# Output projection of a hybrid encoder block: the first product is copied into the residual stream, and its residual is added by the first of three adding DMAs

## The chip, the cores and the metric

The kernel runs on one core of a Trainium2 chip. The metric is the device time of one execution in microseconds (us); lower is better. The engines of the core are named as the profile names them: PE (matrix products), DVE (VectorE), ACT (ScalarE), POOL (GpSimd) and SP (a queue that only issues DMAs).

## What is computed

One layer of an encoder block on 512 tokens with 1024 features, all in float32:

```python
h = rms_norm(x, mix_norm_g)
proj = h @ w_in            # feeds three mixers and their merge gates
merged = g_ml * (y_ml @ w_br_ml) + g_na * (y_na @ w_br_na) + g_xa * (y_xa @ w_br_xa)
x = x + merged @ w_out                                           # the output projection
x = x + conv_glu_ffn(rms_norm(x, ffn_norm_g), w_ffn_up, ...)     # the feed-forward part
return rms_norm(x, final_norm_g)
```

The change lies in the line `x = x + merged @ w_out`: a product of 512x1024 by 1024x1024, the sum with the old `x` (the residual), and the start of the RMS norm that comes next.

## The kernel before, in words

Every float32 product is made of three matmuls (`mm3`, lines 223 to 226): both operands are split into a high and a low part, and high by high, high by low and low by high are summed in PSUM. ACT makes the high part by a copy, DVE the low part by a subtraction. For weights of the other stages these are the pairs at lines 184 and 185; in the output projection they are lines 1238 and 1239 for `w_out` and its sums, and lines 1132 and 1134/1136 for the blocks of `merged`.

The output projection uses seven products instead of eight (Strassen's scheme in Winograd's form). `merged` and `w_out` are cut into two by two blocks; each of the products p1, p5, p2, p6, p3, p7, p4 (`ORDER_O`, in this order) multiplies a sum of blocks of `merged` (256 tokens by 512 features) by a block, or a sum of blocks, of `w_out` (512 by 512). The sums on the weight side were made earlier by DMAs and lie in the tensor `tout`. The sums on the side of `merged` are made in place by DVE (lines 1119, 1121, 1129, 1130). One product is 24 matmuls: four steps `k`, two token tiles `t`, three matmuls each (lines 1438 to 1461).

A product's result is a PSUM tile of 128x1024 (two banks of 512), from a pool of two such tiles (`w2p`, names `at`). The products alternate between the two, so a product may begin only when the result of the product two places ahead of it has been read: p3 begins when p2's result has been read, p4 when p3's has.

The new residual stream lies in two tiles, one for each half of the tokens: `xtu[0]` (named `u_5188` in the rows below) and `xtu[1]` (`u_5189`). `cells((r, c))` is a quarter: token half `r`, feature half `c`, as 128x2x512. The function `wide_adder` builds the quarters. A running sum `Q` starts with p1 and takes p6 and p7. `residual(c)` issues on POOL a DMA that adds a quarter of the old `x` (`xtok` in HBM) to what stands in `cells(c)`. Before the change this goes as follows:

- p1: ACT copies p1 to `Q` (line 1180).
- p5: ACT copies p5 into both quarters of the right half, and POOL issues the adding DMA of each (lines 1186, 1187, 1171).
- p2: DVE writes p2 + `Q` into quarter (0, 0) (line 1182), and POOL then issues that quarter's adding DMA (lines 1183, 1171).
- p6, p3, p7 and p4 follow with sums by DVE (lines 1189, 1191, 1193, 1175, 1163). Quarter (1, 0) takes its `x` by a plain load (line 1422).

Once a token tile is done, ACT forms the sums of its squares in two halves (`squares`, line 1203), DVE adds them (line 1213), POOL takes the power -0.5 (line 1208), ACT scales the tile (`normed`, line 1399, tiles `z`), and PE transposes it for the feed-forward part (`turn`, line 1414). The table `todo` (lines 1428 to 1436) says at which step each of these functions is called: `add("p1")` at step 1 of p5, `add("p2")` at step 1 of p6, `turn(0)` for the first 256 tokens at step 2 of p4. A scheduler then orders the instructions of each engine from its own estimates, so that neighbours on an engine need not stand in the order of the code. Each engine works its list off in order: an instruction that waits holds up all behind it.

Meanwhile SP loads what comes next: the sums in `tout` for p7 and p4 (line 1230), and the first weights of the feed-forward part (`wr<-wflat`, line 160) through a ring of three buffers that it shares with some blocks of `w_out`. ACT splits those weights at line 184.

Of the kernel before, what the change touches and what calls it, by code (L numbers as in the profile page):

```python
# [13 lines left out]
AF = mybir.ActivationFunctionType  # L14
ALU = mybir.AluOpType
# [87 lines left out]
def hybrid_block(ctx, tc, xg, xT, xtok, memT, wflat, wout, wdn, vecs, gbias, nabias, out):  # L103
    nc = tc.nc
    V, A, G, PE, SY = nc.vector, nc.scalar, nc.gpsimd, nc.tensor, nc.sync
# [13 lines left out]
    def nm(s):  # L119
        uid[0] += 1  # L120
        return f"{s}_{uid[0]}"

    def unit(dt=F32):
        return up.tile([P, UNIT], dt, tag="unit", name=nm("u"))
# [7 lines left out]
    def mmps():  # L132
        return mmp.tile([P, 512], F32, tag="mm", name=nm("mm"))
# [271 lines left out]
    def proj(key, XHs, XLs, n=S, at={}, ps=None):  # L405

        ws = weights(key)
        k0 = 0 if ps is None else 1
        if ps is None:
            ps = mmps()  # L410
        for k in range(k0, KT):
            mm3(ps[:, :n], ws[k][0], ws[k][1], XHs[k], XLs[k], k == 0, k == KT - 1)
            if k in (1, 3, 5):
                flush()
            if k in at:
                at[k]()
        return ps
# [63 lines left out]
    for f in range(4):  # L481
        ps = ps_k[f] if f < 2 else proj(("mlk", f), XH, XL)
# [27 lines left out]
    for c in range(3):  # L510
        n, nk = TMC[c], TMK[c]
        pss = [(mmps if c % 2 else atps)() for _ in range(NT)]
        for h in range(KT // nk):
            ws = weights(("tm", c, h))
            for t in range(NT):
                tsl = slice(t * P, (t + 1) * P)
                for k in range(nk):
                    kk = nk * h + k
                    ps = pss[t][:, :n]
                    mm3(ps, XH[kk][:, tsl], XL[kk][:, tsl], ws[k][0], ws[k][1], kk == 0, kk == KT - 1)  # L520
        for t in range(NT):
            ps = pss[t]
# [619 lines left out]
    def cells(c):  # L1142
        return xtu[c[0]][:, :2 * D].rearrange("p (t n) -> p t n", t=2)[:, :, c[1] * S:(c[1] + 1) * S]
# [23 lines left out]
    def wide_adder(banks, Q):  # L1167

        def residual(c):
            r0, c0 = c[0] * 2 * P, c[1] * S  # L1170
            G.dma_start(cells(c), xtok[r0:r0 + 2 * P, c0:c0 + S].rearrange("(t p) n -> p t n", p=P), accum_op=ALU.add)

        def add(name, c=None):
            if c is not None:
                V.tensor_tensor(cells(c), cells(c), Q[0], op=ALU.subtract if c[1] else ALU.add)
                return
            ps = banks[name].rearrange("p (t n) -> p t n", t=2)
            if name == "p1":
                Q.append(unit()[:, :2 * S].rearrange("p (t n) -> p t n", t=2))
                A.activation(Q[0], ps, AF.Copy)  # L1180
            if name == "p2":
                V.tensor_tensor(cells((0, 0)), ps, Q[0], op=ALU.add)
                residual((0, 0))
            if name == "p5":
                for r in range(2):
                    A.activation(cells((r, 1)), ps, AF.Copy)
                    residual((r, 1))
            if name == "p6":
                V.tensor_tensor(Q[0], ps, Q[0], op=ALU.add)
            if name == "p3":  # L1190
                V.tensor_tensor(cells((0, 1)), ps, cells((0, 1)), op=ALU.add)
            if name == "p7":
                V.tensor_tensor(Q[0], Q[0], ps, op=ALU.subtract)

        return add
# [52 lines left out]
    def step(n=1):  # L1248
        quota[0] += n
        while quota[0] >= 1 and gens:  # L1250
            try:
                next(gens[0])
                quota[0] -= 1
            except StopIteration:
                gens.pop(0)
        if not gens:
            quota[0] = 0.0
# [5 lines left out]
    def paced(key, rate=RB):  # L1263
        return proj(key, XH, XL, at={k: lambda: step(rate / 4) for k in (1, 3, 5)})

    xq = unit()
    for f in range(4):
        ps = proj(("xaq", f), XH, XL)
# [3 lines left out]
    for f in range(4):  # L1272
        ps = paced(("o", f), RN if f else RB)
# [15 lines left out]
    for f in range(4):  # L1289
        ps = proj(("memk", f), MH, ML, M, at={3: lambda: step(RM / 2)})  # L1290
# [15 lines left out]
    for f in range(4):  # L1306
        ps = paced(("naq", f), RN)
        V.tensor_tensor(nq[:, f * S:(f + 1) * S].rearrange("p (b r c) -> p b r c", r=ROWS, b=4), rv(ps), rv(rb),
                        op=ALU.mult)
        step(RN / 4)  # L1310
    for f in range(4):
        ps = paced(("nak", f), RN)
# [12 lines left out]
    for br in range(3):  # L1325
# [19 lines left out]
        for fp in range(4):  # L1345
# [16 lines left out]
            for i in range(2):  # L1362
                f = 2 * fp + i
                ps = mmps()
# [236 lines left out]
    banks, Q = {}, []  # L1601
# [196 lines left out]
```

## Time and profile before

| what | value |
|---|---|
| median of 3 runs | 858.2 us (857.5, 858.2, 859.56) |
| the profiled execution's own time | 858.97 us |
| its span in the profile | 857.2 us |
| PE, share of the span busy | 848.3 us, 99% |
| DVE | 622.6 us, 73% |
| ACT | 480.2 us, 56% |
| POOL | 133.0 us, 16% |

The span runs from the first to the last instruction of the program; the profiled execution took 1.8 us more than that. Times in rows of the profile count from the start of the span. A row of the timeline gives start, duration, engine, line, operation, `out<-in`, how many instructions were merged into the row, and in square brackets the idle time of the engine ahead of it with what ended it. The output projection takes from about 460 to 502 us.

### The profile page before, as it was taken

Reading aid. Unit: us, or ns where it says so; the run is one execution under the profiler, and the core shown is the slowest. Engines: PE = TensorE matmul, PEld = TensorE weight load, DVE = VectorE, ACT = ScalarE, POOL = GpSimd, SP = SyncE. Lnnn points to the kernel's source line nnn. Section 1 sums busy time; section 2 is a strip of 40 time slices with the busy share of each in tenths; the row PEclk is TensorE's granted clock in tenths of the full one; section 3 lists DMA queues with packets and bytes.
Section 4 is the critical chain, followed back from the end, with each engine's and each line's share of the span. In section 5 each row is a group of like instructions: output and inputs, shape, how many; then the busy total and the mean of one; then the engine's idle time right before and its main releaser. Section 6 shows DMA issues by size and latency. Waiting matters only on the chain.

```text
span 857.2 us, 12114 instructions
## 1 busy us (share of the span) xinstructions
PE 848.3 (99%) x4175; PEld 716.8 (84%) x4175; DVE 622.6 (73%) x1277; ACT 480.2 (56%) x988; POOL 133.0 (16%) x245
## 2 busy tenths in 40 slices
PE   9999999999999999999999999999999999999996
PEld 7898889988888888888888888888888888888885
DVE  7774698987567758898769967475758666694784
ACT  7663467675446658888735674343434444463463
POOL 0101100010127561600000111030213110001101
PEclk9999999999999999999999999999999999999999
DMA  8233642595664444544442844487869672477942
GB/s 280 81 108 123 185 154 84 158 290 154 179 196 127 114 125 131 157 142 132 146 178 98 221 147 145 152 286 277 262 217 352 203 243 99 135 251 257 381 166 99
DMA packets 53982, 155.00 MB, mean 181 GB/s; under 512 B 6872, under 2 KB 11992, under 8 KB 53344
## 3 DMA queue, kind: packets, MB, share of 16 engines
q1 hardware_dynamic: 30912, 101.37, 34.8%
q0 software_dynamic: 22576, 52.46, 20.8%
q8 instruction: 33, 0.54, 0.3%
q10 hardware_dynamic: 432, 0.39, 0.1%
q14 instruction: 29, 0.24, 0.1%
HBM read 132.68 MB, written 29.90 MB: 190 GB/s over the span
## 4 chain that ended last, share of the span: by engine, by line
PE 94%; DVE 2%; DMA 2%; ACT 1%; issue 1%; POOL 0%; SPq 0%; POOLq 0%
PE mm L224 25%; PE mm L225 25%; PE mm L226 25%; PE at L225 4%; PE at L226 4%; PE at L224 4%; DMA u<-xtok 1%; PE at L990 1%; PE at L971 1%; DVE u L1239 1%; DMA wr<-wflat 0%; PE at L952 0%; PE at L953 0%; PE at L773 0%; PE at L821 0%
## 5 line engine op out<-in xcount | busy, mean ns | idle before, releaser
L224 PE MATMUL mm<-u,wh 128*128 128x512 f32 (+1 forms) x859 | 330.1, 385 | 0.4 <-ACT wh L184 0.3
L225 PE MATMUL mm<-u,wh 128*128 128x512 f32 (+1 forms) x859 | 327.7, 382 | 0.0
L226 PE MATMUL mm<-u,wl 128*128 128x512 f32 (+1 forms) x859 | 327.7, 382 | 0.0
L184 ACT ACTIVATE wh<-wr 128x512 fp32r<-128x512 f32 (+2 forms) x240 | 149.8, 628 | 236.6 <-PE mm L225 198.8
L185 DVE TENSOR_TENSOR wl<-wr,wh 128x512 fp32r<-128x512 f32 (+2 forms) x242 | 164.2, 683 | 84.2 <-ACT wh L184 83.5
L226 PEld LDWEIGHTS mm<-u,wl 128*128 128x128 f32 x859 | 161.4, 188 | 31.4 <-DVE wl L185 0.2
L224 PEld LDWEIGHTS mm<-u,wh 128*128 128x128 f32 x859 | 161.3, 188 | 30.9 <-ACT wh L184 0.7
L225 PEld LDWEIGHTS mm<-u,wh 128*128 128x128 f32 x859 | 161.6, 188 | 30.4 <-DVE u L231 0.4
L548 POOL DMA_DIRECT2D u<-nav_d x128 | 62.7, 531 | 55.6 <-PE at L990 23.0
L1132 ACT ACTIVATE u<-u 128x1024 fp32r<-128x1024 f32 (+1 forms) x28 | 27.5, 998 | 32.0 <-PE mm L226 9.0
L225 PE MATMUL at<-wl,u 128*128 128x512 f32 (+2 forms) x130 | 44.0, 338 | 0.0
L226 PE MATMUL at<-wh,u 128*128 128x512 f32 (+2 forms) x130 | 43.8, 337 | 0.0
L224 PE MATMUL at<-wh,u 128*128 128x512 f32 (+2 forms) x130 | 43.7, 337 | 0.0
L1134 DVE TENSOR_TENSOR u<-u,u 128x1024 fp32r<-128x1024 f32 (+1 forms) x21 | 23.7, 1134 | 13.6 <-ACT u L1132 13.5
L1580 DVE TENSOR_TENSOR u<-mm,s 128x512 f32<-128x512 f32 x22 | 15.2, 689 | 25.1 <-PE mm L226 23.6
L225 PE MATMUL mm<-wl,u 128*128 128x512 f32 x80 | 31.3, 391 | 0.0
L224 PE MATMUL at<-u,u 128*128 128x512 f32 x80 | 31.2, 390 | 0.0
L226 PE MATMUL mm<-wh,u 128*128 128x512 f32 x80 | 31.2, 390 | 0.0
L226 PE MATMUL at<-u,u 128*128 128x512 f32 x80 | 31.1, 389 | 0.0
L225 PE MATMUL at<-u,u 128*128 128x512 f32 x80 | 31.1, 389 | 0.0
L224 PE MATMUL mm<-wh,u 128*128 128x512 f32 x80 | 31.0, 390 | 0.0
L1488 POOL DMA_DIRECT2D tsp<-u x22 | 15.6, 709 | 96.5 <-ACT u L1483 89.1
(365 smaller groups left out, 1333.4 us busy)
## 6 DMA issues: line engine op xcount, KB each, us to landing
wr<-wflat SPq DMA_DIRECT2D x117, 512.0 KB, 3.8
u<-wdn POOLq DMA_DIRECT2D x11, 1024.0 KB, 9.4
tsp<-u POOLq DMA_DIRECT2D x22, 512.0 KB, 6.9
u<-tsp POOLq DMA_DIRECT2D x10, 1024.0 KB, 6.0
tdn<-u POOLq DMA_DIRECT2D x11, 512.0 KB, 6.3
tout<-wout POOLq DMA_DIRECT2D x4, 1024.0 KB, 9.7
nab<-nabias SPq DMA_DIRECT2D x16, 256.0 KB, 2.8
u<-nav_d POOLq DMA_DIRECT2D x128, 32.0 KB, 2.8
```

The source lines that it names most:

```text
L184: A.activation(h[:, u:v], src, AF.Copy)
L185: V.tensor_tensor(l[:, u:v], src, h[:, u:v].bitcast(F32), op=ALU.subtract)
L224: PE.matmul(ps, lh, rh, start=start, stop=False)
L225: PE.matmul(ps, lh, rl, start=False, stop=False)
L226: st["mm"] = PE.matmul(ps, ll, rh, start=False, stop=stop).ins
L548: G.dma_start(vw[r * 32:(r + 1) * 32, i * 256:(i + 1) * 256], nav_v[hf, r, CW[b]:CW[b] + 32, hp * 256:(hp + 1) * 256])
L971: PE.transpose(pt[:, j * P:(j + 1) * P], sm[:, j * P:(j + 1) * P], ident)
L990: PE.matmul(py[:, bl * 256:(bl + 1) * 256], vw[:, c:c + P], pp[bl][:, hf * 256:(hf + 1) * 256], start=hf == 0, stop=hf == 1)
L1132: st["oh"] = A.activation(r3(h), src, AF.Copy, scale=scale).ins
L1134: V.tensor_tensor(r3(l), src, r3(h).bitcast(F32), op=ALU.subtract)
L1488: G.dma_start(tsp[:, x, :, ks].rearrange("q p n -> p q n"), hl[0][:, x])
L1580: V.tensor_tensor(ur, pu, c, op=ALU.mult)
```

## The change

ACT now copies p1 twice: first into quarter (0, 0) of the residual stream, then to `Q` as before. Right behind the first copy that quarter's adding DMA is issued, ahead of the two of the right half. When p2 is done, DVE adds p2 to what stands in the quarter, in place, and no DMA follows.

```diff
             if name == "p1":
                 Q.append(unit()[:, :2 * S].rearrange("p (t n) -> p t n", t=2))
+                A.activation(cells((0, 0)), ps, AF.Copy)
+                residual((0, 0))
                 A.activation(Q[0], ps, AF.Copy)
             if name == "p2":
-                V.tensor_tensor(cells((0, 0)), ps, Q[0], op=ALU.add)
-                residual((0, 0))
+                V.tensor_tensor(cells((0, 0)), ps, cells((0, 0)), op=ALU.add)
```

In the changed kernel the lines behind this place move down by one: the copy to `Q` is line 1182, the sum with p2 line 1184, the copies of p5 line 1187, the splits of `w_out` lines 1239 and 1240, the squares line 1204.

On POOL the adding DMA of quarter (0, 0) now stands ahead of the other two. On SP the two loads of `tout` for p4 now stand ahead of the first load of feed-forward weights, not behind it. PE's list is the same. ACT and DVE are ordered anew in two places. The names in the rows: `u_2700` and `u_2701` are the blocks of `merged`; `u_5312` or `u_5314` and the like are the split parts of `w_out`; `wr_5362` and `wr_5364` before, `wr_5363` and `wr_5365` after, are the first two weight blocks of the feed-forward part in the ring.

ACT before, from the split of p7's first half of weights to the first two sums of squares:

```order
L1238 ACTIVATE u_5312<-wr_5251 128x1024
L184 ACTIVATE wh_5442<-wr_5362 128x512
L184 ACTIVATE wh_5446<-wr_5362 128x512
L1132 ACTIVATE u_5321<-u_2700 128x1024
L1238 ACTIVATE u_5334<-wr_5269 128x1024
L1238 ACTIVATE u_5350<-u_5293 128x1024
L1132 ACTIVATE u_5359<-u_2700 128x1024
L184 ACTIVATE wh_5465<-wr_5364 128x512
L1238 ACTIVATE u_5375<-u_5293 128x1024
L1132 ACTIVATE u_5378<-u_2701 128x1024
L1203 ACTIVATE s_5389,y_5388<-u_5188 128x512
L1203 ACTIVATE s_5392,y_5391<-u_5188 128x512
```

The same stretch of ACT after the change:

```order
L1239 ACTIVATE u_5314<-wr_5253 128x1024
L1132 ACTIVATE u_5323<-u_2700 128x1024
L1239 ACTIVATE u_5335<-wr_5271 128x1024
L1239 ACTIVATE u_5351<-u_5295 128x1024
L1132 ACTIVATE u_5360<-u_2700 128x1024
L184 ACTIVATE wh_5443<-wr_5363 128x512
L184 ACTIVATE wh_5447<-wr_5363 128x512
L184 ACTIVATE wh_5466<-wr_5365 128x512
L184 ACTIVATE wh_5470<-wr_5365 128x512
L1239 ACTIVATE u_5376<-u_5295 128x1024
L1132 ACTIVATE u_5379<-u_2701 128x1024
L1204 ACTIVATE s_5390,y_5389<-u_5188 128x512
```

The four splits of feed-forward weights (line 184) now stand together, ahead of the last two copies for p4 (`u_5376`, `u_5379`). Before, two stood further ahead, one directly ahead of these copies, and the fourth behind the first two sums of squares.

DVE before, from a low part for p6 to the sum with p2 and two more low parts:

```order
L1239 TENSOR_TENSOR u_5234<-wr_5147,u_5234 128x1024
L1239 TENSOR_TENSOR u_5253<-wr_5149,u_5253 128x1024
L1239 TENSOR_TENSOR u_5271<-u_5215,u_5271 128x1024
L1136 SCALAR_TENSOR_TENSOR u_5280<-u_2700,u_5280 128x1024
L1129 TENSOR_TENSOR u_2700<-u_2701,u_2700 128x4x256
L1239 TENSOR_TENSOR u_5295<-u_5215,u_5295 128x1024
L1239 TENSOR_TENSOR u_5312<-wr_5251,u_5312 128x1024
L1130 TENSOR_TENSOR u_2700<-u_2701,u_2700 128x4x256
L1182 TENSOR_TENSOR u_5188<-at_5268,u_5243 128x2x512
L1136 SCALAR_TENSOR_TENSOR u_5321<-u_2700,u_5321 128x1024
L1239 TENSOR_TENSOR u_5334<-wr_5269,u_5334 128x1024
```

The same stretch of DVE after the change:

```order
L1240 TENSOR_TENSOR u_5234<-wr_5147,u_5234 128x1024
L1129 TENSOR_TENSOR u_2700<-u_2701,u_2700 128x4x256
L1240 TENSOR_TENSOR u_5255<-wr_5149,u_5255 128x1024
L1240 TENSOR_TENSOR u_5273<-u_5215,u_5273 128x1024
L1136 SCALAR_TENSOR_TENSOR u_5282<-u_2700,u_5282 128x1024
L1130 TENSOR_TENSOR u_2700<-u_2701,u_2700 128x4x256
L1240 TENSOR_TENSOR u_5297<-u_5215,u_5297 128x1024
L1240 TENSOR_TENSOR u_5314<-wr_5253,u_5314 128x1024
L1136 SCALAR_TENSOR_TENSOR u_5323<-u_2700,u_5323 128x1024
L1184 TENSOR_TENSOR u_5188<-at_5270,u_5188 128x2x512
L1240 TENSOR_TENSOR u_5335<-wr_5271,u_5335 128x1024
```

Two block sums (lines 1129 and 1130) stand earlier. The sum with p2 stands one place later, behind a low part for p3 (`u_5323`). The low parts that free the ring's buffers (`u_5255` and `u_5314`) each stand one place later.

## Prediction

> **What bounds the kernel now.** I began with the page. PE is busy for nearly the whole span and carries nearly the whole chain.
>
> ```profile
> span 857.2 us, 12114 instructions
> PE 94%; DVE 2%; DMA 2%; ACT 1%; issue 1%; POOL 0%; SPq 0%; POOLq 0%
> ```
>
> So the change is worth what it does to PE's waits around 460 to 502 us. The chain through that stretch comes next. Its columns are start, duration and what was waited for.
>
> ```profile
> 478.39 1.15 DVE u L1182
> 479.82 11.79 DMA u<-xtok
> 491.64 1.34 ACT s L1203 x4
> 493.50 0.62 ACT s L1203 x2
> 494.14 0.23 DVE y L1213
> 494.45 0.95 POOL y L1208
> 495.42 1.96 ACT z L1399 x3
> 497.43 1.86 PE mm L1414 x15
> ```
>
> The adding DMA of quarter (0, 0) is issued after DVE's sum with p2 and lands 11.79 us later. Only then do the squares, the power and the scaling run that PE's transposes need. This is the piece that the change pulls forward. What it costs PE today stands in PE's timeline.
>
> ```profile
> 482.35 0.39 PE L224 MATMUL at<-u,u 128*128 128x512 f32 x1
> ...
> 493.23 0.39 PE L224 MATMUL at<-u,u 128*128 128x512 f32 x1
> ...
> 495.72 0.39 PE L226 MATMUL at<-u,u 128*128 128x512 f32 x1
> 496.20 0.33 PE L1414 MATMUL mm<-ident,z 128*128 128x128 f32 x1
> 497.43 1.86 PE L1414 MATMUL mm<-ident,z 128*128 128x128 f32 x15 [0.89 <-ACT z L1399]
> 499.04 0.47 PE L224 MATMUL at<-u,u 128*128 128x512 f32 x1
> ```
>
> 482.35 and 493.23 are the starts of p3 and p4 (24 matmuls of 0.227 us, 5.44 us a product). After half of p4 come the transposes. One runs at 496.20, and the other fifteen wait for `z` until 497.43 and let p4 go on at 499.04. Without a wait the fifteen would begin one transpose (about 0.12 us) after 496.20, and p4 would go on at 496.32 + 1.61 = 497.93. **The most that this change can win here is 499.04 - 497.93 = 1.1 us**, 0.13% of the time. Elsewhere the instruction lists are the same. I take 0.2% (1.7 us) as what a measurement of this kernel tells from no change, so a visible gain isn't to be had.
>
> **The change part by part: ACT's second copy.** ACT's, DVE's and POOL's timelines:
>
> ```profile
> 468.25 1.01 ACT L1180 ACTIVATE u<-at 128x1024 f32<-128x1024 f32 x1
> 472.00 1.92 ACT L1186 ACTIVATE u<-at 128x1024 f32<-128x1024 f32 x2
> 484.98 0.63 ACT L184 ACTIVATE wh<-wr 128x512 fp32r<-128x512 f32 x1 [1.49 <-DMA wr<-wflat]
> 485.51 1.04 ACT L1238 ACTIVATE u<-u 128x1024 fp32r<-128x1024 f32 x1
> ```
>
> ```profile
> 476.04 1.22 DVE L1239 TENSOR_TENSOR u<-wr,u 128x1024 fp32r<-128x1024 f32 x1
> 478.31 1.22 DVE L1182 TENSOR_TENSOR u<-at,u 128x1024 f32<-128x1024 f32 x1
> 486.59 1.23 DVE L1239 TENSOR_TENSOR u<-u,u 128x1024 fp32r<-128x1024 f32 x1
> 490.60 1.22 DVE L1191 TENSOR_TENSOR u<-at,u 128x1024 f32<-128x1024 f32 x1
> 491.74 1.29 DVE L185 TENSOR_TENSOR wl<-wr,wh 128x512 fp32r<-128x512 f32 x2
> 494.14 0.21 DVE L1213 TENSOR_SCALAR y<-y,y 128x1 f32<-128x1 f32 x1 [1.12 <-ACT s L1203]
> ```
>
> ```profile
> 473.31 2.48 POOL L1171 DMA_DIRECT2D u<-xtok  x2 [106.27 <-DMA wr<-tout]
> ```
>
> One more copy like line 1180 takes 0.95 us of ACT's time (two in 1.92 us). Both copies of p1 then end at about 470.2. p2 needs that PSUM tile from 471.46 (two products before 482.35), so 1.2 us are left. The copies of p5 end at 474.9, and p6 needs theirs from 476.9. Both are hidden; if that cover were gone, the cost would be up to 0.95 us of PE.
>
> **The moved DMA.** It is issued about 0.3 us after the first copy of p1, as it was after p5's copy (473.0 to 473.31), so at about 469.6 instead of 479.82. What such a transfer takes:
>
> ```profile
> L1171 POOL DMA_DIRECT2D u<-xtok x3: 1178/1257/1567, 473.3 to 479.8; - x3
> ...
> DMA to landing us min/median/max: 11.8/11.9/14.4
> ```
>
> By the median it would land at 481.5, by the longest at 484.0. Those three met queues that the moved one does not. The traffic in the windows 468 to 472, 472 to 478 and 478 to 485 (packets, MB, busy share of the 16 DMA engines; q1 is SP's queue, q0 is POOL's):
>
> ```profile
> DMA packets 34, 0.14 MB, mean 36 GB/s; under 512 B 0, under 2 KB 0, under 8 KB 33
> ```
>
> ```profile
> q1 hardware_dynamic: 393, 1.45, 76.8%
> ```
>
> ```profile
> q0 software_dynamic: 447, 0.88, 68.6%
> q1 hardware_dynamic: 294, 1.04, 39.4%
> ```
>
> From 468 to 472 hardly anything moves. From 472 to 478 SP's queue keeps the engines 77% busy, while the two adding DMAs that are already issued move nothing. From 478 to 485 both queues share. On q0 0.88 MB took 68.6% of 7 us, so one transfer of 0.52 MB costs 2.9 us of all engines. My estimate is that the moved one lands at 476 to 479. The Trainium skill (DMA: Bandwidth & Descriptors, "Anatomy of one DMA — SWDGE (gpsimd) path") fits such a DMA as 2.0 us plus bytes over 436 GB/s, which makes 3.2 us and a landing at 472.8. The three rows above, at 11.8 to 14.4 us, don't agree, since here it queues behind others.
>
> **The new wait.** DVE's sum with p2 now waits for that landing. Behind it on DVE stand low parts for p7 and p4 and the sum with p6, and PE's p3 needs p2's PSUM tile. In the new order DVE reaches this sum at about 479.4: its rows are spaced 1.13 to 1.15 us, and one row (the low part `u_5323`) now stands ahead of it. A landing before 479.4 costs nothing. The sum takes 1.15 us, so PE waits at 482.35 only if the landing comes after 481.2.
>
> **What is late next.** With the DMA early, the first squares no longer wait for it. They need something else now: ACT must get to them, and the second pair needs DVE's sum with p3 (line 1191). ACT's list now has all four splits of feed-forward weights ahead of `u_5376` and `u_5379`, so ACT waits there for the second weight block. Before, that load went as follows:
>
> ```profile
> 477.29 0.33 SPq L160 DMA_DIRECT2D wr<-wflat  x1
> ```
>
> ```profile
> L160 SPq DMA_DIRECT2D wr<-wflat x1: 333/333/333, 477.3 to 477.3; - x1
> ...
> DMA to landing us min/median/max: 7.7/7.7/7.7
> ```
>
> It landed at 484.95, and ACT's split began at 484.98. From there DVE's sum with p3 ended at 491.82 (490.60 + 1.22), 6.84 us later. After the change two splits, not one, stand ahead of the copy for p4; at 0.53 us a split (485.51 - 484.98) that makes 7.37 us. Call S the time at which the second block's first split begins. The sum with p3 ends at S + 7.37, and the second squares run at once. But DVE has two low parts (1.29 us, 491.74) ahead of the addition of the squares, so it comes 1.25 us later. From that addition to `z` it took 495.42 - 494.14 = 1.28 us. Hence `z` begins at S + 7.37 + 1.25 + 1.28 = S + 9.9, against 495.42 now. **The change gives S - 485.5 us, and never less than -1.1.**
>
> S follows the second block's landing. Its buffer is freed by the low part at 476.04, which now stands one row later, so the load is issued at about 478.35, not 477.29. With the 7.7 us of before it lands at 486.0. The moved DMA bears on this from two sides. It fills idle time: 23% of 6 us are 1.4 us of engine time between 472 and 478. But it also brings POOL's transfers forward into SP's way. If POOL had moved no more than the 0.88 MB that it moved by 485, the 1.4 us would be won: 484.95 - 1.4 = 483.6. If all three were through before the block, 1.57 - 0.88 = 0.69 MB more at 68.6% of 7 us per 0.88 MB cost 3.8 us, less 1.4 us: 487.3. I take 486.0, near the middle, since the issue is later and the queue no shorter.
>
> The sum is 486.0 - 485.5 = +0.5 us, with bounds of -1.1 (483.6 is below the floor) and +1.8. p4's start adds nothing: the sum with p3 would end at 493.4, and p4 starts at 493.23. The profiled execution took 858.97 us with a span of 857.2; I expect a span near 857.7. That execution lay 0.8 us above the median of 858.2, so I add to the median: **858.7 us**.
>
> **The rivals.** *The gain arrives.* The weights land by 484.5, `z` comes before PE asks for it, and the wait at 497.43 goes: -1.0 to -1.1 us, 857.1. For it speaks the idle time from 472 to 478; against it, the later issue of that load. Chance 0.17.
>
> *The weights are held up.* POOL's three transfers all go ahead of the second weight block: it lands after 487.2, the sum with p3 ends after 494.6, p4 starts late, and from there each further microsecond costs one. At 487.7, a little past the bound because of the later issue, it is +2.2 us, 860.4: slower. For it speaks that q0 moved 447 packets beside 294 of q1 when both were full; against it, that DVE's new order frees the ring's buffer only a row later. Decision point 487.2, chance 0.13. The Trainium skill (same page, "Issuing engines are not separate DMA queues") says that DMAs of all issuers run on the same 16 engines and interleave; by that rule, an adding DMA that starts earlier is taken from the weights. The window of 478 to 485 agrees, with both queues in it at 68.6% and 39.4%.
>
> *The new wait on DVE holds PE.* The moved DMA takes 14.4 us as the slowest did and lands at 484.0. The sum ends at 485.2 and p3 starts 2.9 us late. That hides the 1.1 us of before, so +1.8 us, 860.0: slower. It decides from 481.2 on, but up to about 1 us is lost in the later wait for `z`. Against it, the empty engines from 468 to 472. Chance 0.06.
>
> *The DMA isn't what ends the wait at all* is the forecast itself: the 4 us that ACT waits for it today are taken up by the weights.
>
> **How the numbers follow.** The forecast (a landing between 484.5 and 487.2, -1.0 to +1.7 us) has 0.64. The gain is too small to show; I leave 0.05 for faster, for things that these rows don't show, since the floor of -1.1 us is above -1.7. Slower by over 1.7 us: 0.13 + 0.03 (half of the DVE rival). The rest, 0.79, is within 0.2%. The range goes from the floor, 857.0, to the weights held up to 487.7, 860.4.
>
> **What would show it.** In the new profile: the adding DMA issued near 469.6 and landed before 479.4; DVE's sum with p2 (line 1184) without a wait, or with one for `u<-xtok` that ends before 481.2; p3 on PE still near 482.35; ACT waiting at line 184 for `wr<-wflat` until about 486; the first squares (line 1204) without a wait for `u<-xtok`; DVE's sum with p3 (line 1192) ending near 493.4; the transposes still waiting for `z` by about 0.9 to 1.4 us. I am wrong if the transposes don't wait and p4 goes on near 498, if PE waits ahead of p3, or if the weights land outside 484 to 487.

## The result: slower by 0.25%

The changed kernel takes 860.71 us (median of 10 runs, 859.99 to 861.42), the kernel before 858.76 us on the same chips (10 runs, 857.5 to 859.85). The ratio is 1.0025, with a 95% interval of 1.0015 to 1.0034, so the change costs 1.3 to 2.9 us. Forecast were 858.7 us and a range of 857.0 to 860.4; the result lies just outside.

The profiled execution of the changed kernel took 859.99 us, the lowest of its runs. Its page and PE's waits between 440 and 520 us (us in total, times, longest):

```profile
span 858.2 us, 12110 instructions
PE 95%; DVE 3%; DMA 1%; issue 1%; ACT 1%; POOL 0%; POOLq 0%; DVEq 0%
```

```profile
PE at L224 <- DVE u L1192: 1.6, 1, 1.6
PE mm L1415 <- ACT z L1400: 0.9, 1, 0.9
```

The DMA's share of the chain is 1% where it was 2%, but another DMA stands in the chain now (below). The wait for `z` is still there at 0.9 us, and a second one of 1.6 us stands ahead of it. PE's timeline shows both:

```profile
492.49 0.39 PE L226 MATMUL at<-u,u 128*128 128x512 f32 x1
494.53 0.47 PE L224 MATMUL at<-u,u 128*128 128x512 f32 x1 [1.65 <-DVE u L1192]
...
497.56 0.33 PE L1415 MATMUL mm<-ident,z 128*128 128x128 f32 x1
498.78 1.86 PE L1415 MATMUL mm<-ident,z 128*128 128x128 f32 x15 [0.90 <-ACT z L1400]
500.39 0.48 PE L224 MATMUL at<-u,u 128*128 128x512 f32 x1
```

p3's last matmul starts at 492.49, so without a wait p4 would have begun at 492.49 + 0.23 = 492.72. It began at 493.23 in the trace of before, so this trace runs 0.5 us ahead when it comes here, and 0.5 us has to be added to its times to set them beside before's. p4 is 1.8 us late, and the product goes on behind the transposes at 500.39 + 0.5 = 500.9, 1.85 us later than the 499.04 of before. That is the whole loss, within the interval of 1.3 to 2.9 us.

Where the lateness comes from stands in the chain of waits through this stretch (start, duration, what was waited for):

```profile
477.99 9.01 DMA wr<-wflat
...
487.02 0.03 ACT wh L184
...
493.17 1.22 DVE u L1192
494.39 1.20 DVE wl L185 x2
...
496.78 1.96 ACT z L1400 x3
```

In before's chain a row `DMA u<-xtok` of 11.79 us stood here, the adding DMA. Now the load of the second weight block has its place, with 9.01 us. The adding DMA itself does what was asked of it. POOL's row, its landing, and DVE's and ACT's rows:

```profile
469.05 1.26 POOL L1171 DMA_DIRECT2D u<-xtok  x1 [104.07 <-DVE u L1240]
```

```profile
DMA to landing us min/median/max: 9.3/9.3/9.3
```

```profile
479.01 1.22 DVE L1184 TENSOR_TENSOR u<-at,u 128x1024 f32<-128x1024 f32 x1
```

```profile
484.48 1.15 ACT L184 ACTIVATE wh<-wr 128x512 fp32r<-128x512 f32 x2 [3.64 <-DMA wr<-wflat]
487.02 1.15 ACT L184 ACTIVATE wh<-wr 128x512 fp32r<-128x512 f32 x2 [1.39 <-DMA wr<-wflat]
488.08 1.04 ACT L1239 ACTIVATE u<-u 128x1024 fp32r<-128x1024 f32 x1
...
494.42 0.63 ACT L1204 ACTIVATE s<-u 128x512 f32<-128x512 f32 x1 [3.12 <-DVE u L1192]
```

It lands at 469.05 + 9.3 = 478.3, and DVE comes to its sum with p2 (line 1184) at 479.01 without a wait. The squares no longer wait for it. ACT stands still for 3.64 and 1.39 us ahead of the splits of line 184, because the first block lands just ahead of 484.48 and the second at 477.99 + 9.01 = 487.00; and the first copy for p4 (line 1239, 488.08) is queued behind them. DVE's low part for p4 waits for that copy, and its sum with p3 (line 1192) comes behind the low part:

```profile
489.15 1.23 DVE L1240 TENSOR_TENSOR u<-u,u 128x1024 fp32r<-128x1024 f32 x1 [4.39 <-ACT u L1239]
```

### The profile page after: what moved, and what is told of

It reads as the page before. It is cut to its first block, busy times and chain, and to the rows that moved or that the text cites. A ratio compares the mean times of both kernels' runs of the same rounds, so it can differ in the third digit from the quotient of the medians.

```text
span 858.2 us, 12110 instructions
## 1 busy us (share of the span) xinstructions
PE 848.0 (99%) x4175; PEld 716.7 (84%) x4175; DVE 622.7 (73%) x1277; ACT 481.6 (56%) x989; POOL 133.2 (16%) x245
## 4 chain that ended last, share of the span: by engine, by line
PE 95%; DVE 3%; DMA 1%; issue 1%; ACT 1%; POOL 0%; POOLq 0%; DVEq 0%
PE mm L224 25%; PE mm L225 25%; PE mm L226 25%; PE at L225 4%; PE at L226 4%; PE at L224 4%; DMA wr<-wflat 1%; DVE u L1240 1%; PE at L990 1%; PE at L971 1%; DVE u L1136 0%; PE at L952 0%; PE at L953 0%; PE at L773 0%; PE at L821 0%
## 6 DMA issues: line engine op xcount, KB each, us to landing
tout<-wout POOLq DMA_DIRECT2D x4, 1024.0 KB, 10.4
```

## The experiments

The theory after the result: the moved DMA takes the DMA engines from SP's loads, so the second weight block lands 1.5 to 2 us later; ACT's list, in which the splits stand ahead of the operand copies, hands this on to p4. Rivals: the new order on ACT and DVE costs by itself, whatever the DMA does; or the lateness comes from the later issue of the block. Ratios are to the kernel before on the same chip, with 95% intervals.

**The splits behind the copies.** The splits of both blocks are held back until the copies for p4 are issued:

```diff
             if (name, k) == ("p7", 3):
-                ahead_to(ua0 + 2, ua0)
+                after(st["oh"], lambda: ahead_to(ua0 + 2, ua0))
             if (name, k) == ("p4", 1):
-                ahead_to(ua0 + 2, ua0 + 1)
+                after(st["oh"], lambda: ahead_to(ua0 + 2, ua0 + 1))
```

> The changed kernel; only the four splits of feed-forward weights (line 184) are put behind the last two copies for p4 on ACT; DVE, SP, POOL and PE keep their lists. The queue theory (the weights reach PE only because ACT meets their splits ahead of p4's copies, and so DVE's sum with p3 is late): the weights still land near 484.5 and 487.0, but the sum with p3 ends about 1.2 us after p3, the transposes no longer wait, and the kernel is 2.5 to 3 us below the changed kernel and 0.8 to 1.2 us below the kernel before (ratio 0.9986 to 0.999). The rival (something else holds PE, the DMA's or the second copy's contention with the engines): the ratio stays near 1.0025.

Measured: 857.66 us, ratio 0.9990 (0.9981 to 0.9999). ACT's rows, and PE's row at the transposes:

```profile
482.20 1.06 ACT L1239 ACTIVATE u<-u 128x1024 fp32r<-128x1024 f32 x1 [1.15 <-PE at L226]
...
487.02 1.15 ACT L184 ACTIVATE wh<-wr 128x512 fp32r<-128x512 f32 x2 [0.54 <-DMA wr<-wflat]
490.10 0.63 ACT L1204 ACTIVATE s<-u 128x512 f32<-128x512 f32 x1 [1.92 <-DVE u L1192]
...
492.46 2.56 ACT L1400 ACTIVATE z<-u,y 128x512 f32<-128x512 f32 x4 [1.02 <-POOL y L1209]
```

```profile
495.61 1.91 PE L1415 MATMUL mm<-ident,z 128*128 128x128 f32 x16
```

The second block's split begins at 487.02, as late as in the changed kernel. Yet the copy for p4 runs at 482.20 instead of 488.08, `z` is there at 492.46 + 2.56 = 495.02 before PE asks for it at 495.61, and PE waits for nothing between 440 and 520 us. A late block is harmless where nothing for p4 queues behind it. This version is faster than both kernels, than the one before by little: 0.01 to 0.19%.

**The copy without the early DMA.** ACT's and DVE's lists stay those of the changed kernel, but the adding DMA goes out where it did before:

```diff
                 A.activation(cells((0, 0)), ps, AF.Copy)
-                residual((0, 0))
                 A.activation(Q[0], ps, AF.Copy)
             if name == "p2":
                 V.tensor_tensor(cells((0, 0)), ps, cells((0, 0)), op=ALU.add)
+                residual((0, 0))
```

> The changed kernel with ACT's first copy of p1 and DVE's sum in place, but with quarter (0, 0)'s adding DMA issued after the sum with p2, as before the change; ACT's, DVE's and SP's lists are those of the changed kernel. The contention theory (the moved DMA makes the second weight block late): without it the block lands by 485.5 to 486, as in the kernel before, and the time is within 0.6 us of before. The order theory (the block is late because the lists issue it later and behind the loads of tout): it lands at 486.5 to 487.5 as in the changed kernel, and the ratio stays near 1.002 to 1.003.

Measured: 859.51 us, ratio 1.0005 (0.9996 to 1.0014). The load of the second block is issued at 478.2 and takes this long; ACT's split follows:

```profile
DMA to landing us min/median/max: 7.2/7.2/7.2
```

```profile
485.37 1.15 ACT L184 ACTIVATE wh<-wr 128x512 fp32r<-128x512 f32 x2 [2.62 <-DMA wr<-wflat]
```

So the block takes 7.2 us where it takes 9.0 us in the changed kernel, and its split begins at 485.37, not 487.02, though this trace runs some 0.2 us behind that one. The order and the later issue of the block cost nothing that shows, and the early DMA does, though by a narrow margin: this interval ends at 1.0014, and the changed kernel's begins at 1.0015. PE waits only 0.9 us, for `z`. What the DMA engines did between 473.5 and 478 us (packets, MB, busy share), in the changed kernel and then in this one:

```profile
q0 software_dynamic: 272, 0.52, 63.5%
q1 hardware_dynamic: 211, 0.75, 43.2%
```

```profile
q1 hardware_dynamic: 338, 1.26, 91.8%
```

Both moved as much in all, 1.27 and 1.26 MB. The moved transfer's 0.52 MB is, to the rounding, what SP's queue did not move: 1.26 - 0.75 = 0.51 MB.

**Without that quarter's adding DMA.** The line `residual((0, 0))` is left out, so this kernel never adds that quarter of the old `x`.

> The changed kernel without quarter (0, 0)'s adding DMA at all (that quarter of x is not added), so POOL moves 1.0 MB in this stretch instead of 1.57. The contention theory: the second weight block lands at 484 to 485.5, DVE's sum with p3 ends by 493, and the time is 1 to 2 us below the changed kernel. The order theory: it lands at 486.5 to 487.5 and the time is within 0.5 us of the changed kernel.

Measured: 858.87 us, ratio 0.9996 (0.9987 to 1.0004). Against the changed kernel's 1.0025 that is about 2.5 us less, more than the 1 to 2 us expected. ACT's rows:

```profile
485.16 1.15 ACT L184 ACTIVATE wh<-wr 128x512 fp32r<-128x512 f32 x2 [2.45 <-DMA wr<-wflat]
...
492.56 0.63 ACT L1203 ACTIVATE s<-u 128x512 f32<-128x512 f32 x1 [3.12 <-DVE u L1191]
494.92 2.56 ACT L1399 ACTIVATE z<-u,y 128x512 f32<-128x512 f32 x4 [1.02 <-POOL y L1208]
```

With the DMA gone altogether PE still waits 0.9 us for `z`. In this order of ACT's list the DMA that ended the wait before is worth nothing measurable; the second block (485.16) is the next to be late. The block lands as in the run above, so it is the early time of the adding DMA that moves the block, not that there is one.

**The same splits in the kernel before.** The first edit, in the kernel before:

> The kernel before with the four splits put behind the last two copies for p4, and so also behind the first two squares. The queue theory: the first squares wait for the DMA until about 491.6, the splits and the low part ahead of the sum with p3 wait behind them, the sum ends near 495.3 instead of 491.8, and the kernel is 2 to 2.8 us above before (ratio 1.0025 to 1.003). The rival (the place of the splits doesn't matter): ratio 1.000.

Measured: 861.21 us, ratio 1.0023 (1.0014 to 1.0031). ACT's rows, then DVE's:

```profile
491.16 0.63 ACT L1203 ACTIVATE s<-u 128x512 f32<-128x512 f32 x1 [6.51 <-DMA u<-xtok]
...
492.40 2.17 ACT L184 ACTIVATE wh<-wr 128x512 fp32r<-128x512 f32 x4
```

```profile
493.05 0.69 DVE L185 TENSOR_TENSOR wl<-wr,wh 128x512 fp32r<-128x512 f32 x1 [4.21 <-ACT wh L184]
493.66 1.22 DVE L1191 TENSOR_TENSOR u<-at,u 128x1024 f32<-128x1024 f32 x1
```

Here the splits stand behind squares that wait for the late adding DMA. A low part of the weights on DVE waits 4.21 us for them, and the sum with p3 stands behind that. PE is held 1.5 us at p4, almost as in the changed kernel, by another transfer. The gain of the first experiment needs both: the early DMA and the late splits.

**Only the second block's splits behind the copies.** The first of the two edits above is left out.

> The changed kernel; only the two splits of the second weight block are put behind p4's copies on ACT, and the first block's two splits stay ahead of them. The queue theory (the time of the first split that ACT must wait for last ahead of p4's copies sets the end of DVE's sum with p3, 7.4 us later): the first block lands near 484.4, the sum ends near 491.8, before p4 needs it, PE waits for neither the sum nor the transposes' input, and the ratio to before is 0.998 to 0.9995, like the kernel with all four behind. The rival (any weight split ahead of p4's copies costs, or the fast result came from elsewhere): PE still waits, ratio 1.000 to 1.002.

Measured: 858.41 us, ratio 0.9993 (0.9984 to 1.0001). ACT's rows:

```profile
484.57 1.15 ACT L184 ACTIVATE wh<-wr 128x512 fp32r<-128x512 f32 x2 [3.39 <-DMA wr<-wflat]
485.63 1.04 ACT L1239 ACTIVATE u<-u 128x1024 fp32r<-128x1024 f32 x1
...
491.97 0.63 ACT L1204 ACTIVATE s<-u 128x512 f32<-128x512 f32 x1 [2.08 <-DVE u L1192]
494.33 2.56 ACT L1400 ACTIVATE z<-u,y 128x512 f32<-128x512 f32 x4 [1.02 <-POOL y L1209]
```

Now the first block, at 484.57, is what the copy stands behind, and PE waits 0.3 us for `z`, where no wait was expected. The distances are those of the changed kernel: from the block's split to the squares of p3's part 7.40 us (491.97 - 484.57), and there 494.42 - 487.02 = 7.40 us.

**The adding DMA third, first attempt.** `residual((0, 0))` was written behind the loop that issues the other two:

```diff
                 A.activation(cells((0, 0)), ps, AF.Copy)
-                residual((0, 0))
...
                     residual((r, 1))
+                residual((0, 0))
```

> The changed kernel with quarter (0, 0)'s adding DMA issued behind the two of the right half, all else alike; the sum with p2 still waits for it. The queue theory: POOL's three transfers land in order, the third near 489 to 490; DVE's sum with p2 stands from 479 until then, p3 starts near 490.8 instead of 482.3, and the time is 6 to 9 us above before (ratio 1.007 to 1.011). The rival (the moved DMA's place on POOL's queue doesn't matter, since the engines share): it lands before 482 and the ratio stays near 1.002.

Measured: 861.00 us, ratio 1.0024 (1.0013 to 1.0034). This tests nothing that it was meant to. The scheduler issued the DMA first all the same, at 469.5, and every engine's list is that of the changed kernel. It is a second reading of that one, with the block a little later:

```profile
487.92 1.15 ACT L184 ACTIVATE wh<-wr 128x512 fp32r<-128x512 f32 x2 [1.49 <-DMA wr<-wflat]
```

**The adding DMA third, in fact.** Its issue is tied behind the last of the other two:

```diff
-            G.dma_start(cells(c), xtok[r0:r0 + 2 * P, c0:c0 + S].rearrange("(t p) n -> p t n", p=P), accum_op=ALU.add)
+            st["res"] = G.dma_start(cells(c), xtok[r0:r0 + 2 * P, c0:c0 + S].rearrange("(t p) n -> p t n", p=P), accum_op=ALU.add).ins
...
                 A.activation(cells((0, 0)), ps, AF.Copy)
-                residual((0, 0))
...
                     residual((r, 1))
+                after(st["res"], lambda: residual((0, 0)))
```

> The changed kernel with quarter (0, 0)'s adding DMA held behind the two of the right half on POOL's list (the run adding_third did not get there: the scheduler kept it first). DVE's sum with p2 stands two low parts later. The queue theory: the transfers land in order, the third near 489 to 491; the sum with p2 waits on DVE from about 481 until then, p3 starts near 491 instead of 482.3, and, less the 1.1 us that the transposes' wait gives back, the time is 6 to 9 us above before (ratio 1.007 to 1.0105). The second weight block lands near 485.4, as in the run with the copy alone. The rival (the engines share, so the place on POOL's queue doesn't matter): the third lands before 482 and the ratio stays near 1.002.

Measured: 869.86 us, ratio 1.0133 (1.0109 to 1.0156): dearer than expected. DVE's row at the sum with p2, then PE's:

```profile
490.02 1.23 DVE L1183 TENSOR_TENSOR u<-at,u 128x1024 f32<-128x1024 f32 x1 [8.64 <-DMA u<-xtok]
```

```profile
491.40 0.77 PE L224 MATMUL at<-u,u 128*128 128x512 f32 x1 [9.38 <-DVE u L1183]
491.96 0.63 PE L225 MATMUL at<-u,u 128*128 128x512 f32 x1
492.39 0.63 PE L226 MATMUL at<-u,u 128*128 128x512 f32 x1
...
495.64 0.39 PE L225 MATMUL at<-u,u 128*128 128x512 f32 x1
```

The transfer now lands last of the three, at 490.0; the sum with p2 waits for it, and p3 starts 9.4 us late: the prediction's third rival, which the changed kernel escapes only because its DMA goes out first. The rest of the loss goes with the clock. The windows' rows from 482 and from 491 us, with the granted clock in the last column but two:

```profile
482.00:491.00 9.00, 0.01 (x1) 0.00 (x0) 0.97 (x1) 3.04 (x4) 0.00 (x0) 0.68 0.83 206
491.00:496.00 5.00, 4.60 (x12) 3.67 (x13) 5.00 (x6) 1.34 (x4) 0.00 (x0) 0.56 0.00 0
```

After the pause matmuls start 0.43 us apart (492.39 - 491.96) instead of 0.23, until about 495.4. From 491.40 to 495.64 there were ten starts, which take 10 x 0.227 = 2.3 us at full clock and took 4.24 us, 1.9 us more. With the pause of 9.4 us, and without the 0.9 us for `z` that this run doesn't wait, that makes 10.4 us, within the measured 9.4 to 13.4 us. The expectation had left the clock out.

## Why the prediction was wrong, point by point

- **What bounds the kernel, and the most that can be won: right.** PE's waits in this stretch are the whole matter. The version without any wait is 0.1 to 1.6 us faster than before, which agrees with the forecast of 1.1 us at most but doesn't test it closely.
- **ACT's second copy: right.** It is hidden. With the DMA in its old place the ratio is 1.0005, no change by the bound of 0.2%.
- **The moved DMA: right by chance.** Issue at 469.05, 469.55 in before's clock (forecast 469.6), and landing at 478.3 (476 to 479) came out, and the sum with p2 did not wait. The price came out too: 63.5% of the engines for 4.5 us are 2.9 us of all engines. But the landing was argued from the engines' idle time ahead of 472, and the transfer used none of it: it showed no packet for 4.4 us, and then nearly shut out SP's queue (below). Nor did the three transfers of before take their 11.8 to 14.4 us only because they queued behind others; they had such a late start as well (last section).
- **What is late next: right.** The second block's landing took the DMA's place, and the form S + 7.37 and S + 9.9 holds: 487.02 + 7.37 = 494.39, where the sum with p3 ended (493.17 + 1.22), and `z` began at 496.78, 9.76 us after S. In the runs without the early DMA, with S at 485.37 and 485.16, PE waits for `z` as forecast for such an S, and the time is within 0.2%.
- **The landing of the second block: wrong, and this is the step that failed.** The prediction took "the 7.7 us of before", and so let the moved DMA's two effects cancel: that it "fills idle time", 1.4 us, and that it brings POOL's transfers "forward into SP's way". From issue to landing the block took 9.0 us with the early DMA, and 7.2 and 7.0 us without it, with SP's list the same. So the second effect won by 1.8 to 2.0 us. The idle time to fill was about 0.4 us: from 473.5 us, where the moved DMA's first packets show, to 478 SP's queue alone kept the engines 91.8% busy in the run without the early DMA (90.7% in the run without the DMA). Ahead of 473.5 the moved DMA showed no packet; the changed kernel's only large queue from 470 to 473.5 us is SP's:

```profile
q1 hardware_dynamic: 104, 0.43, 58.6%
```

The prediction read its 23% from the trace of before, and that trace is as idle from 473.5 to 478 (first row). But the run of before with the splits moved, where SP's list is that of before, is not (second row):

```profile
q1 hardware_dynamic: 298, 1.10, 77.1%
```

```profile
q1 hardware_dynamic: 319, 1.17, 92.6%
```

So the idle time was one trace's reading, not room that could be counted on. What slowed SP's queue in that one trace isn't known.

- **The sum.** S in before's clock is 487.02 + 0.5 = 487.5, and S - 485.5 gives +2.0 us; the medians differ by 1.95 us. The form was right and its one free term 1.5 us off, nearly all of it in the block's time from issue to landing (9.0 us for 7.7). By the prediction's own sign it was wrong: the weights landed outside 484 to 487, at 487.5 in before's clock.
- **The rival.** "The weights are held up", at 0.13, is what happened: the decision point was 487.2 and the landing came past it, p4 started late. Its "all three" of POOL's transfers ahead of the block was nearly so: the moved one landed at 478.3, the next at 473.72 + 11.0 = 484.7, and only the third at 490.0. POOL's queue moved 0.52 MB by 478 and 0.91 MB more by 487, of 1.57 MB in all. And "DVE's new order frees the ring's buffer only a row later", given as a point against it, moved the issue but spared nothing. The price of 860.4 was good; the chance was too low, because the idle time of one trace was read as room.

The Trainium skill (DMA: Bandwidth & Descriptors, "Queues, rings and completion order") says that each DMA engine takes turns between the queues it has work for, a packet at a time, where a packet is typically about 9 to 17 descriptors. Whether the profile counts such packets or single descriptors, no run here tells. In the profile's count the changed kernel's trace shows even turns from 478 us on. The rows from 480 to 482 us:

```profile
q0 software_dynamic: 103, 0.21, 56.6%
q1 hardware_dynamic: 101, 0.39, 51.8%
```

Ahead of that the count is far from even. From 473.5 to 476 us the rows are

```profile
q0 software_dynamic: 204, 0.42, 91.0%
q1 hardware_dynamic: 54, 0.16, 17.1%
```

while SP's queue had work: by 473.5 it had issued four loads of 0.52 MB and moved 0.43 MB. It isn't peculiar to the early DMA either: in the run without it, POOL's queue moved 192 packets from 480 to 482 us beside 21 of SP's. The moved transfer is 272 of the profile's packets, 17 for each of the 16 engines, so nearly all of it would go through in one turn if these are descriptors; but then the even counts later would be left without a reason. Why the adding transfer gets four packets to one at first stays open.

## What to carry to other kernels

A transfer that is started earlier is paid for by whoever used the DMA engines at that time: look for which queue it displaces, and follow that queue's next load to whoever waits for it. Idle time of the DMA engines that one trace shows isn't room to count on: the same stretch was 77% busy in one trace and 91 to 94% in the four others without the early DMA. ACT worked its list in order, and a copy that was due stood behind splits that waited 3.64 and 1.39 us. So a step that waits for a load belongs behind the steps that the bound engine needs: the same early DMA cost 0.25% with the weight splits ahead of the operand copies and gained 0.1% with them behind. Neither edit was any good alone, so an edit that removes one wait should be tried together with the order that the next wait comes from.

## What the runs showed of the hardware

- Adding DMAs start late. The moved one was issued at 469.05, with no packet of any queue from 465 to 470 us, yet its queue shows none before 473.5, 4.4 us later, and it took 9.3 us for 0.52 MB. What the engines had idle in between stayed idle. A like lag of 4 to 5 us stands where SP's queue is busy: in the run without the early DMA the first adding DMA is issued at 473.88, and the first packet shows between 478.0 and 478.2; in the trace of before it is issued at 473.31, and the first packet shows between 478.2 and 478.4. A plain load from POOL starts sooner: in the changed kernel's trace `u<-wdn` (line 1477) is issued at 507.89, and POOL's queue, without a packet since 491, shows the first between 509.2 and 509.5. What fills the adding DMA's longer time no run shows.
- A pause of 9.4 us on PE costs more than itself: the granted clock was 0.56 in the 5 us behind it, and 1.9 us were lost there (the clock as the cause is read from the row, and wasn't tried by itself). The Trainium skill (TensorE: Matmul & The Clock Gate, "Part 1: The HAM clock gate") says that an idle array falls to half its clock and needs about 3.4 us of work to come back; the trace agrees, with starts 0.43 us apart for about 4 us. The pauses of the changed kernel, 1.65 and 0.90 us, left the clock alone: its row of the same stretch has 1.00.

```profile
491.00:496.00 5.00, 3.35 (x16) 2.48 (x15) 5.00 (x8) 1.63 (x6) 0.20 (x1) 1.00 0.00 0
```
